# Layer 0's attention with VectorE in the program's order, adaLN's loads a slot ahead, and the query rotation cut in three slots

## The chip, the cores and the metric

The kernel runs on one core of one Trainium2 chip. The metric is the device time of one execution in microseconds; smaller is better. A core has five instruction streams that matter here: TensorE (PE, with its weight loads shown apart as PEld), VectorE (DVE), ScalarE (ACT), GpSimd (POOL) and SyncE (SP), which issues nearly all of the DMAs.

## The reference

Two layers of a diffusion transformer over 1024 latent tokens and 256 context tokens of width 1024. Each layer modulates its input with an adaLN vector, mixes tokens, gates, projects, and adds the residual under a layer norm. Layer 0 is multi-head latent attention with 16 heads, layer 1 differential attention. Cut to what this change touches:

```python
shift, scale, gate = adaln(c, ada_w[i], ada_b[i])          # silu(c) @ w + b, also for c_ctx
h = x * (1.0 + scale[:, None, :]) + shift[:, None, :]
# layer 0
q_lat, kv_lat, k_pe, gate = jnp.split(t @ w_in, splits, axis=-1)
q = (rms_norm(q_lat, g_qa) @ w_qb).reshape(bsz, n, 16, 64 + 32)
kv = (rms_norm(kv_lat, g_kva) @ w_kvb).reshape(bsz, n, 16, 64 + 64)
q_pe = apply_rope(q_pe, cos, sin); k_pe = apply_rope(k_pe, cos, sin)   # latent tokens only
o = softmax(q k^T * 96**-0.5) v          # latent queries see 1280 keys, context queries the 256 context keys
x = layer_norm(4**0.25 * x + gate * ((o * silu(gate)) @ out_w), ln_g, ln_b)
```

The adaLN products of layer 1 (2 x 1024 by 1024 x 3072) depend on nothing but the conditioning vectors, so they can be computed at any time before layer 1 needs them.

## The kernel before

The program is written in Python and its instructions are put in order by a planner, which has a cost model, gives earlier instructions the higher priority and lets an engine take a later instruction that is ready when an earlier one isn't. Inside `tc.manual_schedule(engines=...)` the engines named keep the program's order instead; all others are still planned. Before the change, the attention of layer 0 names TensorE alone (`MAN = 'P'`, L36).

Precision is kept by splitting: each operand is a high part and a low part, and a product is three matmuls (`mm3`, L185). `split16` (L180) makes the parts: ScalarE writes the high one, then VectorE the low one from the same source and the high one.

**Ahead of the attention.** The latents are projected (up to about 165 us), then the gates of layer 0 are computed in 40 tiles (`gate_tile`, L284), with a side generator beside them, `beside_gates` (L475): it splits the up-projection weights (`up_weights`, L346, with the key rotation and the column norms `col_norms`, L380, which bound the scores), and then computes four chunks of adaLN (`ada_dve`, L431). From 250 to 282 us the values are made (`prod_v0`, L537), and head 0's keys, queries and first row maxima.

**adaLN on VectorE** (`ada_dve`). A chunk is 512 columns of one layer's weight. For each of eight row blocks SP loads 128 x 512 weights into an `adw` buffer (256 KB, L437), and VectorE adds the block, times a column of the conditioning, into one or two accumulators (L441 for the first block, L443 for the others). Each block is one slot of the generator (`yield`). Then two more slots: TensorE sums an accumulator over the partitions (L450 or L462) and VectorE adds the bias (L452 or L463). The attention's generator `ada` has four chunks of layer 1: two with two accumulators (latent and context) and two with one.

**The attention** (L779 to L797). A head has three blocks of queries: `b` = 0 and 1 with 512 latent queries each, and `b` = 2 with the 256 context queries. A unit (`units0`, L709) is one block of queries against two tiles of 128 keys: five units for each latent block, one for the context block. A unit takes six score matmuls into a pair of PSUM banks (L723 to L725), on ScalarE an exponential and a copy to f16 (L667, L668), on GpSimd the low part by a subtraction (L669, both inputs in SBUF), and two units later (`LAG = 2`) twice twelve value matmuls (L735 to L738), in two parts (`retire(0)`, `retire(1)`). After the last unit of a block `fin` divides by the sum on VectorE (L746, L747).

The softmax needs the row maximum of each query beforehand, in the query operand itself: `max0` (L636) computes it in six slots for a latent block. Four slots each multiply 128 queries by 1024 keys (L647) and reduce them on VectorE (L649, 128 x 1024). The fifth does the context keys (L653, L654) and joins the maxima (`ng`, L655). The sixth turns them into rows by a matmul (L658), and VectorE writes them into the query operand (L659, `qH` for a latent block, `qcH` for the context block). A context block has two slots.

Keys and queries of the next head come from `prod_k` (L588) and `prod_q` (L605). Every second head projects keys and plain queries for two heads; every fourth head (while heads 3, 7 and 11 run) projects the rotated part of the queries for four heads, runs `rope` (L250: a shuffle, two products, a sum on VectorE, each 128 x 1024) and splits it. Copies by SP then place the rows of one head (L599, L600, L631, L632).

`run_step` (L690) weaves all this. For each unit it issues the scores, then the first half of the unit's list of side slots, the first twelve value matmuls, the second half of the list, and the other twelve. The list is made from `sides` in order, each generator with its number of slots per unit. One run is block 0 of a head (five units), a second run blocks 1 and 2 (six units). The scores, maxima and projections all take their PSUM from one tag of three pairs, `pair()` (L91), in turn, so a matmul can wait for the reduce or the exponential that read the same pair last. The last head has two runs of its own, with the loads of the output weight beside them (`load_outw`, L756, VectorE's part in L761).

After the attention come the output projection of layer 0, layer 1's attention and its output, up to 1941 us; the change doesn't touch them.

Of the kernel before, what the change touches and what calls it, by code (L numbers as in the profile page):

```python
# [9 lines left out]
F32 = mybir.dt.float32  # L10
F32R = mybir.dt.float32r
# [6 lines left out]
P = 128  # L18
# [16 lines left out]
WAT = ((1, 4, 8, 12, 15), (24, 28, 33, 38, 42))  # L35
MAN = 'P'  # L36
MAN1 = 'P'
HP = 0
# [15 lines left out]
def hybrid_kernel(  # L54
# [194 lines left out]

    def rope(ps, n, cos, sin, sw, r):  # L250
        dve.stream_shuffle(sw[:, :n], ps, SWAP16)
        dve.tensor_tensor(r[:, :n], ps, cos, op=ALU.mult)
        dve.tensor_tensor(sw[:, :n], sw[:, :n], sin, op=ALU.mult)
        dve.tensor_tensor(r[:, :n], r[:, :n], sw[:, :n], op=ALU.add)
        return r[:, :n]

# [89 lines left out]
    def up_weights(pa):  # L346
# [15 lines left out]
        for c0, n in CHUNKS:  # L362
            c = slice(c0, c0 + n)
            kt = pa.tile([ROPE, 512], F32, tag="kt", name=nm("kt"))
            sp.dma_start(kt[:, :n], kp_d[:, c])
            if c0 < SEQ:
                tabs = []
                for j in range(2):
                    tb = pa.tile([ROPE, 512], F32, tag=f"ktab{j}", name=nm("ktab"))
                    sp.dma_start(tb, cs0[j, :ROPE, c])  # L370
                    tabs.append(tb)
                rope(kt, n, tabs[0], tabs[1], rot(pa, [ROPE, 512], F32, "rsw"), kr[:, c])
            else:
                dve.tensor_copy(kr[:, c], kt[:, :n])
            yield
# [4 lines left out]
        def col_norms(dst, parts, n):  # L380
            wsq = pa.tile([P, 2, 512], F32R, tag="wsq", name=nm("wsq"))
            for c0 in range(0, n, 512):
                for j, f in enumerate(parts):
                    f(wsq[:, j, :], slice(c0, c0 + 512))
                yield
                bk = bank("c")
                for j, f in enumerate(parts):
                    pe.matmul(bk, onr, wsq[:, j, :], start=j == 0, stop=j == len(parts) - 1)
# [16 lines left out]
        for i, n in ((0, KVL), (1, KVL), (2, 4 * QL)):  # L405
# [25 lines left out]
    def ada_dve(tile_, bk_, chunks):  # L431

        for layer, pc in chunks:
            acc = [tile_(f"acc{s}") for s in range(1 if layer and pc > 3 else 2)]
            for k in range(KT):
                w = tile_("adw")
                sp.dma_start(w, ada_w[layer, k * P:(k + 1) * P, pc * 512:(pc + 1) * 512])  # L437
                for s, a_ in enumerate(acc):
                    ck = sc[:, 2 * k + s:2 * k + s + 1]
                    if k == 0:  # L440
                        dve.tensor_scalar_mul(a_, w, ck)  # L441
                    else:
                        dve.scalar_tensor_tensor(a_, w, ck, a_, op0=ALU.mult, op1=ALU.add)  # L443
                yield
# [37 lines left out]
    with spool("p0g") as pg:  # L482
# [14 lines left out]
        for _ in side:  # L497
# [107 lines left out]
    def prod_q(h, b):  # L605
# [3 lines left out]
        if h % 4 == 0 and b != 1:  # L609
# [169 lines left out]
    for h in range(H0):  # L779
        last = h == H0 - 1  # L780
        even, quad = (h + 1) % 2 == 0, (h + 1) % 4 == 0
        if last:
# [4 lines left out]
            run_step(units0(h, 0) + units0(h, 2), [(max0(h, 2), (1, 0, 1)), (max0(h, 1), (0, 1, 1, 1, 2, 1)),  # L787
                                                   (load_outw(oH, oL, lambda: w0("ows")), (1, 2, 2, 2, 1))])
            run_step(units0(h, 1), [])
# [599 lines left out]
```

## Time and profile before

| What | Value |
|---|---|
| median of 3 runs | 1940.24 us (1938.42 to 1947.27) |
| the profiled execution's own time | 1943.4 us |
| its span, first to last instruction | 1941.5 us |
| mean granted TensorE clock | 0.966 |
| TensorE busy in layer 0's attention, 350 to 385 us | 33.90 of 35 us |
| VectorE busy there | 21.73 of 35 us |
| GpSimd busy there | 26.92 of 35 us |

The page of the profile gives busy time by engine, then the span in 40 slices, then the costliest groups of instructions. A row in order of time reads: start, duration, engine, line of the kernel, operation, output <- inputs, shapes, and in brackets the idle time of the engine just before it with what ended it. "x2" at the end of a row says that two instructions are merged in it. A row of the table by windows has, after the window and its length, the busy time of TensorE, its weight loads, VectorE, ScalarE and GpSimd, each with its count of instructions, then the granted clock (1.00 is full speed), the DMA share and GB/s. A row of a group ends with its busy time, the mean of one in ns, and the idle time before them.

### The profile page before, as it was taken

What the parts mean: (1) busy time and instruction counts of PE and PEld (TensorE: products, weight loads), DVE (VectorE), ACT (ScalarE), POOL (GpSimd) and SP (SyncE); (2) the same over time, 40 slices, a digit from 0 to 9 for tenths busy, and PEclk for the clock granted to TensorE, in tenths of its full rate; (3) what the DMA queues carried; (4) which work ended last, traced back from release to release, by engine and by line L of the source; (5) the groups of instructions that cost most, each with busy time, mean ns of one, the idle gap of its engine ahead of it and who ended that gap; (6) DMA issues with size and microseconds to landing.
All of it is one profiled execution on the core that took longest, in us unless ns stands there. A gap on an engine that the chain in (4) does not pass through costs nothing. (4 is left out here: it accounts for less than half of the span.)

```text
span 1941.5 us, 36839 instructions
## 1 busy us (share of the span) xinstructions
PE 1748.3 (90%) x14460; PEld 1348.4 (69%) x14460; DVE 1294.9 (67%) x2211; ACT 1037.9 (53%) x2100; POOL 904.3 (47%) x755
## 2 busy tenths in 40 slices
PE   8889979989899899788889998999999999995997
PEld 2889945656556565566668787878787878783666
DVE  1535577585665758436643868696868787868775
ACT  2532157767677688711114565656666666665331
POOL 2442036757667676756563425242424242416222
PEclk9999989999999999989989999999999999997999
DMA  7345531121211213143233212111111121205331
GB/s 248 106 115 155 170 91 43 41 81 24 75 42 40 62 37 107 34 181 126 93 109 91 62 39 56 47 48 49 51 50 50 44 56 34 58 18 194 105 111 61
DMA packets 116365, 155.40 MB, mean 80 GB/s; under 512 B 14448, under 2 KB 85712, under 8 KB 116192
## 3 DMA queue, kind: packets, MB, share of 16 engines
q1 hardware_dynamic: 110432, 147.80, 25.1%
q10 hardware_dynamic: 5760, 5.25, 0.8%
q8 instruction: 114, 1.87, 0.4%
q14 instruction: 59, 0.48, 0.1%
HBM read 99.18 MB, written 27.08 MB: 65 GB/s over the span
## 5 line engine op out<-in xcount | busy, mean ns | idle before, releaser
L669 POOL TENSOR_TENSOR pl<-p,ph 128x1024 f16<-128x1024 f32 (+1 forms) x176 | 367.6, 2094 | 171.5 <-ACT ph L668 160.0
L1110 ACT ACTIVATE p<-ps_b,mx 128x512 f32<-128x512 f32 (+1 forms) x384 | 232.8, 626 | 46.1 <-DVE mx L1107 45.6
L667 ACT ACTIVATE p<-ps_a,esc 128x1024 f32<-128x1024 f32 (+1 forms) x176 | 189.1, 1074 | 119.9 <-PE ps_a L725 113.1
L649 DVE TENSOR_REDUCE mx<-ps_a 128x1 f32<-128x1024 f32 x128 | 155.1, 1220 | 102.2 <-PE ps_a L647 102.2
L183 DVE SCALAR_TENSOR_TENSOR pl<-ps_b,lcf,ph 128x512 f16<-128x512 f32 (+1 forms) x192 | 123.4, 657 | 110.7 <-ACT ph L182 109.3
L668 ACT CAST ph<-p 128x1024 f16<-128x1024 f32 (+1 forms) x176 | 177.1, 1006 | 5.5
L1104 DVE TENSOR_REDUCE mx<-ps_b 128x1 f32<-128x512 f32 x256 | 165.9, 677 | 0.3 <-PE ps_b L1088 0.2
L186 PE MATMUL ps_b<-h1H,wH 128*128 128x512 f32 (+1 forms) x384 | 150.0, 391 | 17.8 <-ACT p L1110 16.1
L738 PE MATMUL ps_d<-Vh,pl 128*128 128x65 f16 x1344 | 150.8, 195 | 7.4 <-POOL pl L669 6.1
L186 PE MATMUL ps_b<-wH,h1H 128*128 128x256 f32 x512 | 156.2, 305 | 0.0
L735 PE MATMUL ps_d<-Vh,ph 128*128 128x65 f16 x1344 | 154.2, 196 | 0.0
L737 PE MATMUL ps_d<-Vl,ph 128*128 128x64 f16 x1344 | 152.7, 193 | 0.0
L187 PE MATMUL ps_b<-wL,h1H 128*128 128x256 f32 x512 | 146.5, 286 | 0.0
L188 PE MATMUL ps_b<-wH,h1L 128*128 128x256 f32 x512 | 146.4, 286 | 0.0
L182 ACT ACTIVATE ph<-ps_b,lcf 128x512 f16<-128x512 f32 (+1 forms) x192 | 120.5, 640 | 41.3 <-PE ps_b L1123 41.3
L188 PE MATMUL ps_b<-h1H,wL 128*128 128x512 f32 (+1 forms) x384 | 139.1, 362 | 3.4 <-POOL wL L178 3.4
L178 POOL TENSOR_TENSOR wL<-ws,wH 128x512 fp32r<-128x512 f32 x64 | 91.3, 1428 | 106.5 <-PE ps_b L187 59.0
L735 PEld LDWEIGHTS <-ph 128*128 128x128 f16 x1344 | 124.6, 98 | 22.6 <-issue 5.6
L187 PE MATMUL ps_b<-h1L,wH 128*128 128x512 f32 (+1 forms) x384 | 138.5, 361 | 0.0
L737 PEld LDWEIGHTS <-ph 128*128 128x128 f16 x1344 | 125.2, 99 | 16.0 <-issue 0.3
L723 PE MATMUL ps_a<-qH,KH 100*128 100x512 f16 x320 | 123.0, 384 | 13.4 <-DVE qH L659 7.6
L1087 PE MATMUL ps_b<-KS,QS 128*128 128x512 f16 (+1 forms) x384 | 128.9, 353 | 3.6 <-ACT p L1110 2.5
(344 smaller groups left out, 5424.1 us busy)
## 6 DMA issues: line engine op xcount, KB each, us to landing
adw<-in_ada_w SPq DMA_DIRECT2D x64, 256.0 KB
ws<-in_dw SPq DMA_DIRECT2D x64, 256.0 KB
g<-sg_d SPq DMA_DIRECT2D x18, 512.0 KB
adaw<-in_ada_w SPq DMA_DIRECT2D x16, 512.0 KB
sg_d<-gg ACTq DMA_DIRECT2D x40, 128.0 KB
o<-o_d SPq DMA_DIRECT2D x10, 512.0 KB
o_d<-op SPq DMA_DIRECT2D x7, 640.0 KB
xt<-in_xT SPq DMA_DIRECT2D x16, 256.0 KB
```

Of the source, the lines that this page charges most:

```text
L186: pe.matmul(ps, aH, bH, start=start, stop=False, skip_group_check=skip)
L187: pe.matmul(ps, aH, bL, start=False, stop=False, skip_group_check=skip)
L188: pe.matmul(ps, aL, bH, start=False, stop=stop, skip_group_check=skip)
L649: dve.tensor_reduce(mx[:, t, 0:1], ps, axis=AX.X, op=ALU.max)
L667: act.activation(p32[:, :n], st, AF.Exp, scale=esc0)
L668: act.copy(ph[:, :n], p32[:, :n])
L669: pool.tensor_tensor(pl[:, :n], p32[:, :n], ph[:, :n], op=ALU.subtract)
L735: pe.matmul(pv[:, t, :], ph[:, ts], Vh[:, k, h, :], start=(k == kcs[0] and t == 0), stop=False, skip_group_check=True)
L737: pe.matmul(pv[:, t, :V0], ph[:, ts], Vl[:, k, h, :], start=False, stop=False, skip_group_check=True)
L738: pe.matmul(pv[:, t, :], pl[:, ts], Vh[:, k, h, :], start=False, stop=(k == NT - 1), skip_group_check=True)
L1104: dve.tensor_reduce(mx[:, 2 + 2 * m + i:3 + 2 * m + i], b, axis=AX.X, op=ALU.max, negate=True)
L1110: act.activation(p[m][:, c0:c0 + n], b, AF.Exp, bias=nb, scale=sc1, accum_out=sm[:, 2 + 3 * m + i:3 + 3 * m + i])
```

## The change

- `MAN0 = 'PD'`: in the two runs of heads 0 to 14 VectorE too keeps the program's order. The last head's runs, and everything outside the runs, keep `MAN`.
- `ada_dve` loads one block ahead: a first slot only loads, and each later slot issues the load of the next block before it computes on its own. `adw` has three buffers instead of two in the attention.
- In both runs `ada` moves from the first to the last place of `sides`. In the third unit of the first run and the third and fifth of the second, its slot so comes after the maxima, and the first half of the list holds a maximum slot more.
- `rope` becomes a generator with two slots: shuffle and first product, then second product and sum. With the split behind them the rotated queries take three slots; the units of heads 3, 7 and 11 get (2, 2, 2, 1, 1) slots of `kq` instead of (2, 2, 2, 0, 0), so that plain queries are projected in the fourth unit and copied in the fifth (before: both in the third).
- In `up_weights`, `col_norms` takes single tiles of 512 columns in two buffers instead of one tile of two; the table buffers of the key rotation grow from 512 to 640 columns, and the low half of the rotated keys is staged in one of them.

```diff
+MAN0 = 'PD'
...
     def rope(ps, n, cos, sin, sw, r):
+
         dve.stream_shuffle(sw[:, :n], ps, SWAP16)
         dve.tensor_tensor(r[:, :n], ps, cos, op=ALU.mult)
+        yield
         dve.tensor_tensor(sw[:, :n], sw[:, :n], sin, op=ALU.mult)
         dve.tensor_tensor(r[:, :n], r[:, :n], sw[:, :n], op=ALU.add)
-        return r[:, :n]
+        yield
...
-                    tb = pa.tile([ROPE, 512], F32, tag=f"ktab{j}", name=nm("ktab"))
+                    tb = pa.tile([ROPE, 640], F32, tag=f"ktab{j}", name=nm("ktab"))[:, :512]
...
-            wsq = pa.tile([P, 2, 512], F32R, tag="wsq", name=nm("wsq"))
             for c0 in range(0, n, 512):
-                for j, f in enumerate(parts):
-                    f(wsq[:, j, :], slice(c0, c0 + 512))
+                wsq = [pa.tile([P, 512], F32R, tag="wsq", bufs=2, name=nm("wsq")) for _ in parts]
+                for w_, f in zip(wsq, parts):
+                    f(w_, slice(c0, c0 + 512))
...
-        kl_ = pa.tile([P, 2, 512], F32R, tag="wsq", name=nm("wsq")).rearrange(
-            "p a b -> p (a b)").bitcast(F16)[:ROPE, :NTOK]
+        kl_ = pa.tile([ROPE, 640], F32, tag="ktab1", name=nm("ktab")).bitcast(F16)
...
-        for layer, pc in chunks:
+        def load(i):
+            layer, pc = chunks[i // KT]
+            k = i % KT
+            w = tile_("adw")
+            sp.dma_start(w, ada_w[layer, k * P:(k + 1) * P, pc * 512:(pc + 1) * 512])
+            return w
+
+        ahead = [load(0)]
+        yield
+        for i, (layer, pc) in enumerate(chunks):
             acc = [tile_(f"acc{s}") for s in range(1 if layer and pc > 3 else 2)]
             for k in range(KT):
-                w = tile_("adw")
-                sp.dma_start(w, ada_w[layer, k * P:(k + 1) * P, pc * 512:(pc + 1) * 512])
+                if i * KT + k + 1 < len(chunks) * KT:
+                    ahead.append(load(i * KT + k + 1))
+                w = ahead.pop(0)
...
-            "ows": ([P, D], F32, 2), "adw": ([P, 512], F32, 2), "acc0": ([P, 512], F32, 1),
+            "ows": ([P, D], F32, 2), "adw": ([P, 512], F32, 3), "acc0": ([P, 512], F32, 1),
...
-                src = rope(src, pn, cosA, sinA, w0("rsw"), w0("rr"))
+                rr = w0("rr")
+                yield from rope(src, pn, cosA, sinA, w0("rsw"), rr)
+                src = rr
...
-    def run_step(units, sides):
-
-        with tc.manual_schedule(engines={ENG[c] for c in MAN}):
+    def run_step(units, sides, man_=MAN0):
+
+        with tc.manual_schedule(engines={ENG[c] for c in man_}):
...
             kq = chain(prod_k(h + 1), prod_q(h + 1, 0))
-            run_step(units0(h, 0), [(ada, (0, 0, 1)), (max0(h, 1), (1, 1, 2, 1, 1)), (max0(h, 2), (0, 1, 0, 1)),
-                                    (kq, (2, 2, 1 + quad, 0, 0) if even else (2,))])
+            run_step(units0(h, 0), [(max0(h, 1), (1, 1, 2, 1, 1)), (max0(h, 2), (0, 1, 0, 1)),
+                                    (kq, ((2, 2, 2, 1, 1) if quad else (2, 2, 1)) if even else (2,)),
+                                    (ada, (0, 0, 1))])
             qs = chain(prod_q(h + 1, 1), prod_q(h + 1, 2))
-            run_step(units0(h, 1) + units0(h, 2), [(ada, (0, 0, 1, 0, 1)), (max0(h + 1, 0), (1, 1, 1, 2, 1)),
-                                                   (qs, (1, 1 + quad, 0, 1) if even else (2,))])
+            run_step(units0(h, 1) + units0(h, 2), [(max0(h + 1, 0), (1, 1, 1, 2, 1)),
+                                                   (qs, (1, 1 + quad, 0, 1) if even else (2,)),
+                                                   (ada, (0, 0, 1, 0, 1))])
```

The last head's two calls pass `MAN`.

More of the change, by code (lines that the diff above doesn't have):

```diff
@@ L368, in up_weights @@
                 for j in range(2):
-                    tb = pa.tile([ROPE, 512], F32, tag=f"ktab{j}", name=nm("ktab"))
+                    tb = pa.tile([ROPE, 640], F32, tag=f"ktab{j}", name=nm("ktab"))[:, :512]
                     sp.dma_start(tb, cs0[j, :ROPE, c])
                     tabs.append(tb)
-                rope(kt, n, tabs[0], tabs[1], rot(pa, [ROPE, 512], F32, "rsw"), kr[:, c])
+                for _ in rope(kt, n, tabs[0], tabs[1], rot(pa, [ROPE, 512], F32, "rsw"), kr[:, c]):
+                    pass
             else:
@@ L380, in col_norms @@
         def col_norms(dst, parts, n):
-            wsq = pa.tile([P, 2, 512], F32R, tag="wsq", name=nm("wsq"))
             for c0 in range(0, n, 512):
-                for j, f in enumerate(parts):
-                    f(wsq[:, j, :], slice(c0, c0 + 512))
+                wsq = [pa.tile([P, 512], F32R, tag="wsq", bufs=2, name=nm("wsq")) for _ in parts]
+                for w_, f in zip(wsq, parts):
+                    f(w_, slice(c0, c0 + 512))
                 yield
                 bk = bank("c")
-                for j, f in enumerate(parts):
-                    pe.matmul(bk, onr, wsq[:, j, :], start=j == 0, stop=j == len(parts) - 1)
+                for j, w_ in enumerate(wsq):
+                    pe.matmul(bk, onr, w_, start=j == 0, stop=j == len(parts) - 1)
                 dve.tensor_reduce(vm[:, 6:7], bk, axis=AX.X, op=ALU.max)
@@ L787, in hybrid_kernel @@
             run_step(units0(h, 0) + units0(h, 2), [(max0(h, 2), (1, 0, 1)), (max0(h, 1), (0, 1, 1, 1, 2, 1)),
[L788 to L789 removed]
+                                                   (load_outw(oH, oL, lambda: w0("ows")), (1, 2, 2, 2, 1))], MAN)
+            run_step(units0(h, 1), [], MAN)
         else:
             kq = chain(prod_k(h + 1), prod_q(h + 1, 0))
[L792 to L793 removed]
+            run_step(units0(h, 0), [(max0(h, 1), (1, 1, 2, 1, 1)), (max0(h, 2), (0, 1, 0, 1)),
+                                    (kq, ((2, 2, 2, 1, 1) if quad else (2, 2, 1)) if even else (2,)),
+                                    (ada, (0, 0, 1))])
             qs = chain(prod_q(h + 1, 1), prod_q(h + 1, 2))
[L795 to L796 removed]
+            run_step(units0(h, 1) + units0(h, 2), [(max0(h + 1, 0), (1, 1, 1, 2, 1)),
+                                                   (qs, (1, 1 + quad, 0, 1) if even else (2,)),
+                                                   (ada, (0, 0, 1, 0, 1))])
     flush()
```

## The prediction

> **What bounds the kernel now.** I read the page first, then the table of busy time by windows, then the order of time on TensorE and VectorE in layer 0's attention.
>
> ```profile
> PE 1748.3 (90%) x14460; PEld 1348.4 (69%) x14460; DVE 1294.9 (67%) x2211; ACT 1037.9 (53%) x2100; POOL 904.3 (47%) x755
> 250.00:282.00 32.00, 23.76 (x97) 16.64 (x97) 24.83 (x26) 18.75 (x20) 12.62 (x7) 0.89 0.34 99
> 350.00:385.00 35.00, 33.90 (x406) 21.87 (x404) 21.73 (x31) 28.49 (x28) 26.92 (x15) 1.00 0.17 45
> 404.00:408.00 4.00, 3.82 (x26) 2.03 (x26) 3.25 (x4) 1.51 (x2) 1.33 (x1) 0.60 0.31 94
> ```
>
> TensorE is the bound (90% of the span). The change reaches the gates' stage (up to 250 us), its end (250 to 282) and the attention (282 to about 815). In a good stretch of the attention TensorE is busy 33.9 of 35 us at full clock; at the stage's start it has 23.8 of 32 at clock 0.89. In order of time, the long waits of TensorE there name VectorE:
>
> ```profile
> 277.79 0.60 PE L653 MATMUL ps_a<-KH,qH 96*128 96x256 f16 x4 [2.02 <-DVE mx L649]
> 280.84 0.27 PE L658 MATMUL ps_a<-idr,ng 128*4 128x128 f32 x1 [2.46 <-DVE ng L655]
> 404.18 0.38 PE L723 MATMUL ps_a<-qH,KH 100*128 100x512 f16 x1 [2.85 <-DVE qH L659]
> ```
>
> What VectorE did in front of them is adaLN, in bursts. A first chunk has run by 307, then comes nothing of it for 88 us, then the next chunk:
>
> ```profile
> 303.86 3.28 DVE L443 SCALAR_TENSOR_TENSOR acc<-adw,sc,acc 128x512 f32<-128x512 f32 x2
> 395.27 0.87 DVE L441 TENSOR_SCALAR acc<-adw,sc 128x512 f32<-128x512 f32 x2
> L443 DVE SCALAR_TENSOR_TENSOR acc<-adw,sc,acc x98: 714/747/2675, 168.3 to 644.7; 128x512 f32<-128x512 f32 x98
> L443 DVE SCALAR_TENSOR_TENSOR acc<-adw,sc,acc 128x512 f32<-128x512 f32 x39 | 46.1, 1197 | 7.3 <-DMA adw<-in_ada_w 7.1
> ```
>
> So the planner fills every idle moment of VectorE with steps that the program meant for later heads, and row maxima wait behind them. A head's pace shows in the times at which its query rows get their maxima (L659: qcH is once a head, qH twice):
>
> ```profile
> 281.48 0.74 DVE L659 SCALAR_TENSOR_TENSOR qH<-ps_a,sh,selt 4x512 f16<-4x512 f32 x1
> 331.67 0.47 DVE L659 SCALAR_TENSOR_TENSOR qcH<-ps_a,sh,selt 2x256 f16<-2x256 f32 x1
> 360.23 0.48 DVE L659 SCALAR_TENSOR_TENSOR qcH<-ps_a,sh,selt 2x256 f16<-2x256 f32 x1
> 399.54 0.48 DVE L659 SCALAR_TENSOR_TENSOR qcH<-ps_a,sh,selt 2x256 f16<-2x256 f32 x1
> 436.58 0.48 DVE L659 SCALAR_TENSOR_TENSOR qcH<-ps_a,sh,selt 2x256 f16<-2x256 f32 x1
> 469.15 0.48 DVE L659 SCALAR_TENSOR_TENSOR qcH<-ps_a,sh,selt 2x256 f16<-2x256 f32 x1
> 497.67 0.48 DVE L659 SCALAR_TENSOR_TENSOR qcH<-ps_a,sh,selt 2x256 f16<-2x256 f32 x1
> 545.14 0.48 DVE L659 SCALAR_TENSOR_TENSOR qcH<-ps_a,sh,selt 2x256 f16<-2x256 f32 x1
> 560.84 0.74 DVE L659 SCALAR_TENSOR_TENSOR qH<-ps_a,sh,selt 4x512 f16<-4x512 f32 x1 [0.41 <-PE ps_a L658]
> 607.03 0.47 DVE L659 SCALAR_TENSOR_TENSOR qcH<-ps_a,sh,selt 2x256 f16<-2x256 f32 x1
> 637.91 0.47 DVE L659 SCALAR_TENSOR_TENSOR qcH<-ps_a,sh,selt 2x256 f16<-2x256 f32 x1
> 676.63 0.48 DVE L659 SCALAR_TENSOR_TENSOR qcH<-ps_a,sh,selt 2x256 f16<-2x256 f32 x1
> 705.90 0.48 DVE L659 SCALAR_TENSOR_TENSOR qcH<-ps_a,sh,selt 2x256 f16<-2x256 f32 x1
> 739.26 0.48 DVE L659 SCALAR_TENSOR_TENSOR qcH<-ps_a,sh,selt 2x256 f16<-2x256 f32 x1
> 771.05 0.48 DVE L659 SCALAR_TENSOR_TENSOR qcH<-ps_a,sh,selt 2x256 f16<-2x256 f32 x1
> ```
>
> The qcH rows are heads 1 to 14, a few left out. An even head takes 28.5 us undisturbed (469.15 to 497.67, 331.67 to 360.23), an odd one 32.6 (436.58 to 469.15), the one after a rotation 29.3 (676.63 to 705.90), and one that makes rotated queries without a burst 38.7 (637.91 to 676.63).
>
> **What goes: the bursts.** Against those paces: the stretch 281.48 to 331.67 is 50.2 us, the same kind of stretch without adaLN (560.84 to 607.03) 46.2: 4.0. Head 4 (399.54 to 436.58) has 37.0 for 29.3: 7.7. Head 7 (497.67 to 545.14) has 47.5 for 38.7: 8.8, part of it a slow clock. Head 10 (607.03 to 637.91) has 30.9 for 28.5: 2.4. Ahead of 282 the two waits of 2.02 and 2.46 stand directly behind adaLN; in program order none of it can come before head 0, so 4.0 of these 4.5 go. Sum 26.9, between 22.9 (without the stage's start) and 27.4. Head 14 (739.26 to 771.05) has 31.8 for 28.5, filled with the last head's weight splits (L761); these stay with the planner, but it may no longer slip them between VectorE's fixed instructions. Between 0 and 3.3, I take 1.5. **Gain 28.4 us.**
>
> **What comes: the same steps, spread.** adaLN's 41 slots now lie three to a head, in heads 0 to 13: (a) third unit of the first run, (b) third and (c) fifth unit of the second. Sixteen slots compute on two accumulators, sixteen on one, the rest are loads, matmuls or empty. In order, each stands between two row maxima. What it costs there, from head 2, which has no adaLN now, and from one adaLN step that met GpSimd:
>
> ```profile
> 508.34 2.67 DVE L443 SCALAR_TENSOR_TENSOR acc<-adw,sc,acc 128x512 f32<-128x512 f32 x1
> 508.34 2.12 POOL L669 TENSOR_TENSOR pl<-p,ph 128x1024 f16<-128x1024 f32 x1 [0.32 <-ACT ph L668]
> 356.07 2.35 DVE L649 TENSOR_REDUCE mx<-ps_a 128x1 f32<-128x1024 f32 x2 [0.50 <-PE ps_a L647]
> 358.02 2.13 POOL L669 TENSOR_TENSOR pl<-p,ph 128x1024 f16<-128x1024 f32 x1 [0.59 <-ACT ph L668]
> 358.97 1.23 DVE L654 TENSOR_REDUCE mx<-ps_a 128x4 f32<-128x1024 f32 x1 [0.54 <-PE ps_a L653]
> 361.04 0.24 PE L658 MATMUL ps_a<-idr,ng 128*4 128x128 f32 x1
> 361.46 0.20 PE L738 MATMUL ps_d<-Vh,pl 128*128 128x65 f16 x1
> L655 DVE TENSOR_REDUCE ng<-mx 128x4 fp32r<-128x8 f32 x31 | 5.0, 160 | 0.9
> 657.11 1.23 DVE L649 TENSOR_REDUCE mx<-ps_a 128x1 f32<-128x1024 f32 x1 [3.05 <-PE ps_a L647]
> ```
>
> A step of 0.75 us (median above) took 2.67, because GpSimd's subtraction started with it: it ended 0.55 after GpSimd did (510.46). Now place (a). The two maxima of the unit end at 358.42; GpSimd runs from 358.02 to 360.15. The step behind the maxima would end at 360.70, with two accumulators at 361.45. The maximum that stands at 358.97 starts then and, with 0.16 us for the joined maximum (L655), lets TensorE have L658 at 362.1 or 362.85 instead of 361.04: 1.0 or 1.8 us. That is for an even head; an odd one has its maximum later, behind a query projection, and I take half. By the slots' count (a) has five double steps (heads 1, 2, 4, 5, 6) and three single ones outside the rotating heads (8, 9, 12): 0.9+1.8+1.8+0.9+1.8+1.0+0.5+1.0 = 9.7. In (b) only one maximum is ahead, the step meets the end of GpSimd's work; I take 0.5 for each of five double steps, 2.5. In (c) VectorE has nothing urgent behind it: before the next head's first maximum it is idle for 3.05 us (row 657.11), which hides even a double step; nothing, and a full step if that idle time were gone. Moving adaLN last also moves the joined maximum's matmul in the second run ahead of twelve value matmuls, 0.42 us by the rows 361.04 and 361.46, fifteen times: between 0 and 6, mostly lent, as TensorE would do the twelve anyway; I take 1. **Cost 13 us**, from 0 (all of it in idle time) to 46.1 (the group row's whole busy time).
>
> The loads a slot ahead come at least two units before use, some 5 us (11 units in 28.5 us). Today's waits for them are 7.3 us of VectorE's idle time in the bursts (the L443 group), counted there already. On SP's queue a load is still one issue per step, now earlier by a slot; with three buffers the one it overwrites was read two slots before, so SP does not stand and the copies of queries and keys behind it (L631, L599) go on time: nothing, and at most those same waits if a load came late. The splits of keys and plain queries wait for ScalarE in order too, and the maxima, `fin` and their buffers queue behind them; in the undisturbed odd head of 32.6 us these stand in the same order, so I take 0. In the gates' stage the planner still orders VectorE, and the split `wsq`, the larger `ktab` and adaLN's extra first slot lie beside the gates' matmuls: nothing, and one step of 0.75 us if these were gone.
>
> **The rotation in three slots** (heads 3, 7, 11). Now in head 11:
>
> ```profile
> 668.83 1.23 DVE L254 TENSOR_TENSOR rr<-rr,rsw 128x1024 f32<-128x1024 f32 x1
> 669.15 2.92 POOL L669 TENSOR_TENSOR pl<-p,ph 128x1024 f16<-128x1024 f32 x1 [3.64 <-ACT ph L668]
> L183 DVE SCALAR_TENSOR_TENSOR stpL<-rr,qsc,stpH 128x1024 f16<-128x1024 f32 x3 | 5.4, 1809 | 0.0
> 670.09 1.15 ACT L182 ACTIVATE stpH<-rr,qsc 128x1024 f16<-128x1024 f32 x1 [1.08 <-DVE rr L254]
> 675.57 0.38 PE L723 MATMUL ps_a<-qH,KH 100*128 100x512 f16 x1
> ```
>
> Today the four rotation steps run in a row, L254 ends at 670.06. In order, two maxima (2.35) come between its halves; the second half then starts at 670.0, meets GpSimd's 2.1 us from 669.15 and so ends near 673.4 (671.3 and two steps of a little over 1 us behind it). Then the in-order queue waits for ScalarE's 1.15 (stpH), to 674.6, splits (1.8 by the group's mean, most of it GpSimd's lock; I take 1.7), to 676.3, takes a single adaLN step in heads 7 and 11, to 677.0, and only then the maximum (1.23) whose buffer the scores of the fifth unit need: 678.3 for 675.57 today, 2.8 later; 2.1 in head 3. In all **7.7 us**. The other way, if the maxima ahead of the rotation free TensorE sooner, it is 0; the other end adds a clock fall: after the 2.85 us wait at 404.18 the clock is 0.60 over 4 us, 1.6 us lost, three times, 12.5. I take 7.7, the rows' own sum.
>
> [...]
>
> **Sum:** -28.4 + 13.2 + 7.7 = -7.5 us. The profiled execution is 1943.4 (span 1941.5 and 1.9 around it), so 1935.9; it lies 3.2 above the median of 1940.24, and for the median I say **1933**.
>
> **Rivals.** *The spread is free:* the steps and the rotation fall into VectorE's idle time, as places (c) do. For it: VectorE is busy 21.7 of 35 us in the good window; against it: place (a)'s rows. Costs 0: 1940.2-28.4 = **1912**. *In single file it is slower:* at (a) and (b) each step's whole time lands on the maximum behind it, GpSimd's subtraction and VectorE's step excluding each other in every unit. Ten double and nine single steps there at 1.2 us an accumulator are 35 us, with the rotation's upper end 47.5, less 28.4: +19, **1959**. It decides once the costs pass 28.4. For it: GpSimd is busy 26.9 of 35 us; against it: today's bursts cost 26.9 us for 46.1 us of steps. [...] *The order hardly changes:* the planner already had nearly this order and the bursts' time is the rotation's: **1940**. Against it: 88 us without a step.
>
> **Chances.** Forecast 0.45 (1924 to 1942), free 0.27, single file 0.20, no change 0.08. A measurement of this kernel tells about 0.5% from no change, 9.7 us: 1930.5 to 1949.9. Of the forecast 0.20 lies below that, 0.25 inside. Faster 0.20+0.27 = 0.47; same 0.25+0.08+0.02 = 0.35; slower 0.18. The range reaches from 1910, just under the free case, to 1955, which leaves out the upper part of single file.
>
> **What would show it.** Right: L443 of the attention spread over heads 0 to 13, no two steps of different slots adjacent; L441 after 282; head 4 near 29 to 31 us; clock near 1.0 where it is 0.60 now; L658 waits of 1 to 2 us in heads 1 to 6; in the rotating heads one wait of 2 to 4 us of L723 for L654. Wrong: heads 2 and 6 still at 28.5 (free), or all heads from 1 to 12 two us longer (single file), or rotating heads above 42.

## The result and the profile after

The change makes the kernel slower: 1957.14 us (median of 5, 1951.97 to 1960.06) against 1941.18 for the kernel before beside it, a ratio of 1.0070 (95% interval 1.0043 to 1.0097). The forecast was 1933, range 1910 to 1955. The profiled execution took 1952.52 us (span 1950.4), near the low end of the five; its mean clock is 0.964, and that of the three executions above 1957 is 0.960 to 0.962.

On the page TensorE's busy time is what it was, within 2.4 us; the span is 8.9 longer.

```profile
PE 1750.7 (90%) x14460; PEld 1345.5 (69%) x14460; DVE 1302.0 (67%) x2211; ACT 1038.6 (53%) x2100; POOL 904.8 (46%) x755
```

The pace by heads, in order of time on VectorE. L659 is now L674 (the lines behind the new ones shift: L443 is L456, L658 is L673, L723 is L738, L761 is L776). As in the prediction, "head n" is the stretch that ends in its qcH row; the rows are those of heads 1 to 8 and 11 to 14, behind the first qH:

```profile
274.77 0.74 DVE L674 SCALAR_TENSOR_TENSOR qH<-ps_a,sh,selt 4x512 f16<-4x512 f32 x1 [0.45 <-PE ps_a L673]
...
323.19 0.48 DVE L674 SCALAR_TENSOR_TENSOR qcH<-ps_a,sh,selt 2x256 f16<-2x256 f32 x1
353.93 0.48 DVE L674 SCALAR_TENSOR_TENSOR qcH<-ps_a,sh,selt 2x256 f16<-2x256 f32 x1
396.03 0.48 DVE L674 SCALAR_TENSOR_TENSOR qcH<-ps_a,sh,selt 2x256 f16<-2x256 f32 x1
431.25 0.48 DVE L674 SCALAR_TENSOR_TENSOR qcH<-ps_a,sh,selt 2x256 f16<-2x256 f32 x1
469.05 0.48 DVE L674 SCALAR_TENSOR_TENSOR qcH<-ps_a,sh,selt 2x256 f16<-2x256 f32 x1
500.06 0.48 DVE L674 SCALAR_TENSOR_TENSOR qcH<-ps_a,sh,selt 2x256 f16<-2x256 f32 x1
542.12 0.48 DVE L674 SCALAR_TENSOR_TENSOR qcH<-ps_a,sh,selt 2x256 f16<-2x256 f32 x1
574.92 0.48 DVE L674 SCALAR_TENSOR_TENSOR qcH<-ps_a,sh,selt 2x256 f16<-2x256 f32 x1
...
676.98 0.48 DVE L674 SCALAR_TENSOR_TENSOR qcH<-ps_a,sh,selt 2x256 f16<-2x256 f32 x1
711.20 0.48 DVE L674 SCALAR_TENSOR_TENSOR qcH<-ps_a,sh,selt 2x256 f16<-2x256 f32 x1
743.67 0.48 DVE L674 SCALAR_TENSOR_TENSOR qcH<-ps_a,sh,selt 2x256 f16<-2x256 f32 x1
781.80 0.47 DVE L674 SCALAR_TENSOR_TENSOR qcH<-ps_a,sh,selt 2x256 f16<-2x256 f32 x1
```

Two cuts, at the first qH and at the qcH of head 13, divide a span in three:

| Kernel | until the first qH | heads 0 to 13 | from there to the end | span |
|---|---|---|---|---|
| before | 281.48 | 457.78 | 1202.2 | 1941.5 |
| the change | 274.77 | 468.90 | 1206.7 | 1950.4 |
| difference | -6.7 | +11.1 | +4.5 | +8.9 |
| forecast | -4.0 | -2.0 | -1.5 | -7.5 |

The bursts did go (heads 4 and 7: 35.2 and 42.1 us for 37.0 and 47.5), but heads 2, 3, 5, 6, 8, 12 and 14 became longer, head 5 by 5.2 us, head 12 by 5.0 and head 14 by 6.3 (1, 9 and 11 by less than 1). By the prediction's own signs: heads 3 and 7 take 42.1 us, just above its line of 42 for the heads that make rotated queries, and head 4 takes 35.2 where 29 to 31 would have been right; but by no means all heads from 1 to 12 are two us longer.

Two kinds of wait are new. TensorE's rows: L673 waits for the joined maximum (0.86 to 1.79 us seven times between 323 and 712, of which two rows stand here, and twice 2.4), and in each rotating head (3, 7 and 11) the scores wait for L669.

```profile
354.04 0.22 PE L673 MATMUL ps_a<-idr,ng 128*4 128x128 f32 x1 [1.62 <-DVE ng L670]
370.93 0.22 PE L673 MATMUL ps_a<-idr,ng 128*4 128x128 f32 x1 [2.43 <-DVE ng L670]
395.85 0.38 PE L738 MATMUL ps_a<-qH,KH 100*128 100x512 f16 x1 [2.84 <-DVE mx L669]
446.61 0.22 PE L673 MATMUL ps_a<-idr,ng 128*4 128x128 f32 x1 [2.45 <-DVE ng L670]
500.17 0.22 PE L673 MATMUL ps_a<-idr,ng 128*4 128x128 f32 x1 [1.79 <-DVE ng L670]
541.95 0.38 PE L738 MATMUL ps_a<-qH,KH 100*128 100x512 f16 x1 [3.24 <-DVE mx L669]
676.80 0.59 PE L738 MATMUL ps_a<-qH,KH 100*128 100x512 f16 x1 [3.52 <-DVE mx L669]
```

And the clock. The table by windows, with the granted clock in the third number from the end, shows from head 1 on five short falls and one long, all but one (516 to 520) at the end of such a wait or right behind it (another fall is under way when head 0 starts, at clock 0.50 until 280.42 us, as it is before, until 288.71):

```profile
355.00:359.00 4.00, 3.88 (x26) 1.94 (x25) 0.69 (x2) 1.39 (x2) 1.96 (x1) 0.57 0.14 37
396.00:400.00 4.00, 4.00 (x34) 2.27 (x33) 2.51 (x3) 1.87 (x2) 0.00 (x0) 0.57 0.18 46
447.00:452.00 5.00, 5.00 (x58) 3.43 (x54) 2.88 (x3) 1.35 (x3) 2.85 (x2) 0.66 0.17 32
516.00:520.00 4.00, 4.00 (x36) 2.72 (x35) 2.15 (x7) 1.30 (x2) 2.67 (x2) 0.58 0.02 4
543.00:548.00 5.00, 5.00 (x55) 3.09 (x54) 2.06 (x3) 2.93 (x3) 2.13 (x1) 0.66 0.36 100
676.00:684.00 8.00, 7.20 (x50) 3.60 (x50) 3.52 (x6) 2.64 (x3) 2.06 (x1) 0.57 0.32 80
```

A window's length times one less its clock is what it lost: 4 x 0.43 = 1.7 us for a short fall, 8 x 0.43 = 3.4 for the long one, 11.9 in all. Before, heads 1 to 13 lost 6.8 in three falls (391 to 395, 404 to 409, 517 to 525).

### The profile page after: what moved, and what is told of

It is laid out like the page before. It is cut to its first block, busy times and chain, and to the rows that moved or that the text cites. A ratio compares the mean times of both kernels' runs of the same rounds, so it can differ in the third digit from the quotient of the medians.

```text
span 1950.4 us, 36828 instructions
## 1 busy us (share of the span) xinstructions
PE 1750.7 (90%) x14460; PEld 1345.5 (69%) x14460; DVE 1302.0 (67%) x2211; ACT 1038.6 (53%) x2100; POOL 904.8 (46%) x755
## 5 line engine op out<-in xcount | busy, mean ns | idle before, releaser
L738 PE MATMUL ps_a<-qH,KH 100*128 100x512 f16 x320 | 125.7, 393 | 15.2 <-DVE mx L669 9.6
```

## The experiments

Each ratio is to the kernel before, timed on the same chip; times of different groups are compared through these ratios.

**Which part of the change is it?** First the theory that the fixed order makes the loss, from both sides.

`order alone`: the kernel before with VectorE in order in heads 0 to 14.

```diff
-    def run_step(units, sides):
+    def run_step(units, sides, man_='PD'):
-        with tc.manual_schedule(engines={ENG[c] for c in MAN}):
+        with tc.manual_schedule(engines={ENG[c] for c in man_}):
```

> The kernel before with the fixed order alone: VectorE in the program's order in heads 0 to 14, adaLN first in a unit with its load in its own slot, the rotation in one slot. Theory: adaLN's steps stand ahead of the maxima, wait for their own load too, and the rotation's four steps stand in a row, so it is as slow as the change or slower, 1957 to 1985 us. Rival (the order is harmless, the other parts cost): 1935 to 1945.

1948.44 us, ratio 1.0000 (0.9984 to 1.0016). `planned`: all of the change but the order (`MAN0 = 'P'`).

> The changed kernel with one letter taken back: VectorE is planned again in the runs of heads 0 to 14, all else of the change stays. Theory (the fixed order costs: adaLN's steps meet GpSimd's subtraction between two row maxima, the rotation's chain holds up the maximum behind it): adaLN runs in bursts again and the time goes back to 1930 to 1945 us. Rival (the load ahead, the third buffer, the lists of side slots or the rotation's slots cost it, the order does not): it stays at 1950 to 1960.

1956.97 us, 1.0050 (1.0029 to 1.0071). So the order by itself is neutral as a whole, and the rest of the change is slow without it: my first theory fell. In the planned run the bursts are back, up to six steps in a row, and the second run of units of each rotating head starts 2.9 us late, as the scores wait for the query rows. A burst on VectorE, then TensorE in head 7:

```profile
423.27 5.94 DVE L456 SCALAR_TENSOR_TENSOR acc<-adw,sc,acc 128x512 f32<-128x512 f32 x6
```

```profile
549.43 0.39 PE L738 MATMUL ps_a<-qH,KH 100*128 100x512 f16 x1 [2.93 <-DVE qH L674]
```

`rotation alone`: the kernel before with the rotation in three slots and nothing else.

```diff
         dve.tensor_tensor(r[:, :n], ps, cos, op=ALU.mult)
+        yield
         dve.tensor_tensor(sw[:, :n], sw[:, :n], sin, op=ALU.mult)
...
-                                    (kq, (2, 2, 1 + quad, 0, 0) if even else (2,))])
+                                    (kq, ((2, 2, 2, 1, 1) if quad else (2, 2, 1)) if even else (2,))])
```

> The kernel before with the rotation of queries in three slots and the new numbers of slots, and nothing else of the change; VectorE stays planned. Theory R (the rotation's slots are what makes the planned version slow): the plain queries are projected one unit later in heads 3, 7 and 11, so the second run of heads 3, 7 and 11 begins with a wait of about 2.9 us on each of three rows, as the run with the planned order showed, plus a clock fall of 1.7 after each: 3 x (2.9 + 1.7) = 14 us slower, ratio 1.006 to 1.008. Rival L (adaLN's place in the list and its loads ahead make it slow): ratio 0.999 to 1.002, the three waits under 1 us.

1956.94 us, 1.0052 (1.0032 to 1.0071), as much as the whole planned run. Heads 4, 8 and 12 take 43.1, 34.9 and 33.5 us for 37.0, 29.3 and 29.3 before. Two of the three waits are there at the size expected, the first is 1.65. VectorE in head 11 shows why: the planner puts a maximum between the two steps of the rotation's second half, both meet GpSimd (2.24 and 2.60 us for steps of 1.2), and the plain queries, now projected a unit later, are split behind them.

```profile
683.69 2.24 DVE L254 TENSOR_TENSOR rsw<-rsw,sinA 128x1024 f32<-128x1024 f32 x1
685.85 1.21 DVE L658 TENSOR_REDUCE mx<-ps_a 128x4 f32<-128x1024 f32 x1
686.99 2.60 DVE L255 TENSOR_TENSOR rr<-rr,rsw 128x1024 f32<-128x1024 f32 x1
...
692.00 1.28 DVE L183 SCALAR_TENSOR_TENSOR stqL<-ps_a,qsc,stqH 128x1024 f16<-128x1024 f32 x1
693.31 0.74 DVE L663 SCALAR_TENSOR_TENSOR qH<-ps_a,sh,selt 4x512 f16<-4x512 f32 x1
```

`adaLN last alone`: the kernel before with `ada` last in both lists.

> The kernel before with adaLN last in the lists of the units in place of first, and nothing else of the change; VectorE stays planned. Theory L: the bursts of L443 move behind maxima and meet a unit's start, waits of about 3 us as at 279 and 295 us in the run with the planned order, ratio 1.004 to 1.008. Theory R: with VectorE planned the place in the list is only a priority, ratio 0.998 to 1.002.

1945.58 us, 1.0004 (0.9987 to 1.0021): with VectorE planned, the place in the list changes nothing that these runs can tell.

**In the fixed order, which part?** `rotation undone`: the change with `rope` in one slot and (2, 2, 1 + quad, 0, 0). `adaLN first`: the change with `ada` first in both lists again.

> The change with the rotation of queries in one slot again and the old numbers of slots; the order, adaLN's last place and the loads ahead stay. Theory P (in the fixed order adaLN's place alone costs): 1.006 to 1.008, as the change. Theory R (the rotation's slots alone cost): 0.999 to 1.001, as the run with the order alone. Both parts: 1.002 to 1.005, with heads 4, 8 and 12 some 2 us each below the change's 35.2, 32.8 and 34.2, and the waits of L673 of 1.6 and 2.4 us in heads 2, 4 and 6 kept.

> The change with adaLN first in the units' lists again, all else kept. Theory P: 0.999 to 1.001, waits of 0.9 to 1.3 us of L668 in heads 1 to 6 in place of L673's 0.9 to 2.4. Theory R: 1.006 to 1.008. Both parts: 1.002 to 1.005.

Rotation undone: 1951.06 us, 1.0023 (1.0005 to 1.0041). adaLN first: 1949.28 us, 1.0008 (0.9995 to 1.0022). Each alone brings back most of the 0.7%, so neither theory of one cause holds. The two parts cost more together (0.0070) than the sum of what each costs alone in this order (0.0023 and 0.0008); the excess of 0.4% is hardly larger than what the three intervals leave open (0.35%). One place where they meet is the last step of this chain, the change's head 11 on VectorE: behind the split stands an adaLN step, and only then the maximum for which the scores wait.

```profile
668.50 2.10 DVE L256 TENSOR_TENSOR rsw<-rsw,sinA 128x1024 f32<-128x1024 f32 x1
...
673.09 1.86 DVE L184 SCALAR_TENSOR_TENSOR stpL<-rr,qsc,stpH 128x1024 f16<-128x1024 f32 x1 [1.22 <-ACT stpH L183]
674.88 0.74 DVE L456 SCALAR_TENSOR_TENSOR acc<-adw,sc,acc 128x512 f32<-128x512 f32 x1
675.54 1.21 DVE L669 TENSOR_REDUCE mx<-ps_a 128x4 f32<-128x1024 f32 x1
```

That wait is 3.52 us in the change and 2.83 with adaLN first, where the step is not in the chain:

```profile
672.58 0.58 PE L738 MATMUL ps_a<-qH,KH 100*128 100x512 f16 x1 [2.83 <-DVE mx L669]
```

**What does the place of adaLN's steps cost?** `idle places`: the change with the steps in the fifth unit of the first run and the fifth and sixth of the second. `first run idle` and `second run idle` take one line of it each.

```diff
-                                    (ada, (0, 0, 1))])
+                                    (ada, (0, 0, 0, 0, 1))])
...
-                                                   (ada, (0, 0, 1, 0, 1))])
+                                                   (ada, (0, 0, 0, 0, 1, 1))])
```

> The change with adaLN's three slots of a head moved to where VectorE idles: the fifth unit of the first run, the fifth and sixth of the second, each behind the last slot of the maxima. Theory (the waits of 1 to 2.4 us of L673 and the clock falls behind them come from the places between maxima): 10 to 16 us less than the change, 1941 to 1947. Rival (the rotating heads and head 14 alone make the loss): 1952 to 1957.

> The change with adaLN's slot of the first run moved from the third to the fifth unit; the second run's two slots stay. Both moved gave 0.9926 where the change has 1.0070: 1.44% or 28 us to share. By the prediction's sizes (9.7 us for the first run's slot, 2.5 for the second run's) four fifths of it go here: 0.995 to 0.997, and the waits of 2.4 us of L673 in heads 2 and 4 stay. Rival, that the second run's double steps, each met by two of GpSimd's operations, cost more than the first run's: 1.000 to 1.004.

> The change with adaLN's slots of the second run moved from the third and fifth to the fifth and sixth unit; the first run's slot stays. By the prediction's sizes: 1.003 to 1.005, with waits of 0.9 to 1.8 us of L673 in heads 1 to 12 kept and the two of 2.4 us gone. Rival: 0.995 to 0.999.

Idle places: 1934.40 us, 0.9926 (0.9908 to 0.9944), faster than the kernel before. First run's slot moved alone: 1936.80, 0.9963 (0.9949 to 0.9976). Second run's alone: 1949.10, 1.0016 (1.0003 to 1.0030). Of the change's 1.0070 the first takes 1.07% or 21 us, the second 0.54% or 10, both together 1.44% or 28, where 10 to 16 had been expected; the change's own interval, 5 us either way, goes into each of these. The place of these steps is the largest single cost. In the idle places, four steps run one after the other where VectorE would stand, and the even head behind takes 29.07 us:

```profile
440.97 5.68 DVE L456 SCALAR_TENSOR_TENSOR acc<-adw,sc,acc 128x512 f32<-128x512 f32 x4
...
460.67 0.48 DVE L674 SCALAR_TENSOR_TENSOR qcH<-ps_a,sh,selt 2x256 f16<-2x256 f32 x1
489.74 0.48 DVE L674 SCALAR_TENSOR_TENSOR qcH<-ps_a,sh,selt 2x256 f16<-2x256 f32 x1
```

**The rotation's slots in the fixed order.** `rotation later` is the change with (2, 2, 1, 2, 1) in place of (2, 2, 2, 1, 1); the other two have the idle places as well, one with the rotation undone, one with the rotation later.

> The change with the split of the rotated queries moved from the third to the fourth unit of heads 3, 7 and 11, behind that unit's maximum. Theory (the scores of the fifth unit wait 2.8 to 3.5 us for the maximum behind that split, and the clock falls after it): these three waits shrink to about 1 us and 6 to 12 us go, 1945 to 1951. Rival (VectorE is simply full there, so the wait moves to the query rows): 1954 to 1959.

> The change with adaLN's steps in the fifth units (0.9926) and the rotation in one slot. If the rotation's slots cost half a per cent in the fixed order too: 0.987 to 0.990. If they cost only with VectorE planned: 0.992 to 0.994, the rotating heads with waits of 3.5 us of the scores for the row maxima as in the run with the order alone.

> The change with adaLN's steps in the fifth units and the rotation's fourth unit given the second slot; the last head as in the change. In the run with these two and the last head in order, the attention's last head began 12.7 us earlier than with the places alone, 6 us of it by head 14, and the last head and what follows took 11.7 us more: without the ordered last head 6 to 7 us of it stay: ratio 0.988 to 0.991, some 1925 where the kernel before has 1944. If the two don't add, 0.9926 stays.

Rotation later: 1953.64, 1.0023 (1.0002 to 1.0044), 9 us less than the change by the ratios and so within the first theory's 6 to 12, though the two intervals leave some 6 us either way. Idle places with the rotation undone: 1930.90, 0.9915 (0.9890 to 0.9940), not to be told from 0.9926. Idle places with the rotation later: 1927.25, 0.9905 (0.9888 to 0.9922), the lowest ratio, called the best version from here on, although its interval overlaps those of 0.9915 and 0.9926. The scores of the rotating heads no longer wait for a maximum but for the query rows, and only 1.64 to 1.66 us, as here in head 7.

```profile
528.20 0.38 PE L738 MATMUL ps_a<-qH,KH 100*128 100x512 f16 x1 [1.64 <-DVE qH L674]
```

**The last heads.** Head 14's 6.3 us stand behind the output weight's splits, which the planner slips between VectorE's fixed instructions. VectorE and TensorE in the change:

```profile
760.04 2.96 DVE L776 SCALAR_TENSOR_TENSOR oL<-ows,usc,oH 128x1024 fp32r<-128x1024 f32 x1
```

```profile
763.22 0.27 PE L673 MATMUL ps_a<-idr,ng 128*4 128x128 f32 x1 [3.78 <-DVE ng L670]
```

`last ordered` is the change with the last head's two calls without `MAN`; `all three` has the idle places, the rotation later and this; `splits last` has them too, with the splits' slots in the last run.

```diff
-                                                   (load_outw(oH, oL, lambda: w0("ows")), (1, 2, 2, 2, 1))], MAN)
-            run_step(units0(h, 1), [], MAN)
+                                                   ])
+            run_step(units0(h, 1), [(load_outw(oH, oL, lambda: w0("ows")), (2, 2, 2, 1, 1))])
```

> The change, with the last head's two runs in the program's order on VectorE as well. If the six us that head 14 lost (38.13 against 31.79) come from the last head's splits, which the planner slips between head 14's fixed instructions, they go: 1957 less 4 to 8, a ratio to the kernel before of 1.002 to 1.005, and head 14 at 32 us. If head 14 is slow by its own order, the time stays at 1.007.

> The change with adaLN's steps in the fifth units (the run of that name was 0.9926), the rotation's fourth unit given the second slot (0.995 against the change), and the last head in order. If the three add: the first gave 0.9926, the second takes some 5 us, the third 4 to 8: 1918 to 1926 where the kernel before has 1941, ratio 0.988 to 0.992. If they lie beside one another, 0.9926 stays.

> The change with adaLN's steps in the fifth units, the rotation's second slot in the fourth unit (0.9905 together), and the last head in the program's order on VectorE with the splits of the output weight moved into its last run, behind all row maxima. If head 14's lost time is these splits standing between maxima, it goes and does not come back in the last head as with the last head in order alone: 6 to 10 us less than 0.9905, so 0.985 to 0.988, head 14 near 29.5 us and no wait of L673 over 2 us in the last head. If the splits then hold up the projection behind the attention by their 13 to 20 us: 0.993 to 0.998.

Last ordered: 1962.01, 1.0076 (1.0058 to 1.0094). All three: 1935.63, 0.9942 (0.9922 to 0.9961). Splits last: 1927.35, 0.9910 (0.9892 to 0.9928). None of the three brought the time that it was to bring. In the first, head 14 takes 29.6 us for 38.1, so the splits were what held it up, and the last head loses as much: its own maxima now wait behind the splits, TensorE 6.41 us in one place:

```profile
817.00 0.27 PE L673 MATMUL ps_a<-idr,ng 128*4 128x128 f32 x1 [6.41 <-DVE ng L670]
```

With the splits behind all maxima head 14 takes 31.7, and in the last run value matmuls wait 2.13 us for GpSimd. GpSimd itself had waited for ScalarE's copy, and ScalarE had stood 1.80 us for a load of the output weight, ahead of its own part of the splits:

```profile
793.26 1.15 ACT L775 ACTIVATE oH<-ows,usc 128x1024 fp32r<-128x1024 f32 x1 [1.80 <-DMA ows<-in_out_w]
797.76 0.24 PE L753 MATMUL ps_d<-Vh,pl 128*128 128x65 f16 x1 [2.13 <-POOL pl L684]
```

From the end of head 13 to the end of the span it is 1203.2 us there and 1202.7 without it (idle places with the rotation later), so nothing is won: in each of the places tried, something waits for the splits or their loads.

## Why the prediction was wrong

It went wrong in both large terms. If the best version (span 1922.0, all of the change but two sets of slots) is taken for the change without its costs, the profiled executions split the result: the change wins 19.5 us (1941.5 - 1922.0) and loses 28.4 (1950.4 - 1922.0), +8.9; the forecast had 28.4 won and 20.9 lost, -7.5.

Where the time of heads 0 to 13 goes can be added up. The waits are the sum of the brackets of TensorE's rows, the clock loss is length times one less the granted clock, here with the fall at the start of head 0. In all seventeen traces what is then left is 413.8 to 417.1 us, so these two make the differences:

| Kernel | heads 0 to 13 | TensorE's waits | clock lost |
|---|---|---|---|
| before | 457.8 | 30.7 | 10.4 |
| order alone | 463.9 | 36.1 | 12.0 |
| the change | 468.9 | 38.8 | 14.8 |
| idle places | 450.6 | 29.0 | 7.6 |
| the best version | 444.8 | 24.8 | 6.2 |

- **What goes: the bursts (28.4 us), the step that failed first.** They went, as the heads show, and heads 0 to 13 should have become 22.9 us shorter without the new costs. The best version's are 12.9 shorter (444.84 us), and those of the order alone, where the bursts are gone too, 6.1 longer (463.90). The step took the paces of the planner's undisturbed heads (28.5, 29.3, 32.6) for what every head would have. In the fixed order they are not all reached even with adaLN in idle places: heads 5, 8 and 12 take 34.4, 31.6 and 31.7 us (9 takes 33.0). Of the 41.1 us of waits and lost clock before, the best version keeps 31.0; the forecast needed some 18. The order alone has 48.1. In it the waits for joined maxima behind the bursts (L658, 9.0 us) are gone, but the product with the context keys (L653) and the scores (L723) wait 18.6 us for row maxima, 7.7 before, and a projection waits 4.0 us at 394.83 for adaLN's bias step (L452), which stands behind the rotation's split. So the fixed order, with adaLN's steps in it, has a price about as large as the bursts', which agrees with 1.0000 for the order alone. The prediction's "so I take 0" for the splits that wait in order was too low as well, by little: TensorE's waits for tiles of the splits and the rotation (`stkL`, `stqL`, `rr`) sum to 6.7 us in the change and 4.1 before. In the idle places 1.2 to 1.3 us of wait for a row maximum is left in each of heads 3 and 5 (behind the four steps shown above in head 5), and the rotating heads' waits.
- **The start.** Forecast -4.0, measured -6.7 in this pair of executions. The matmul that waits 3.4 us for the split of head 0's keys starts at 245.60 instead of 250.59, so 5.0 of the 6.7 arose ahead of 250, in the gates' stage, which I had taken at nothing. But single executions scatter here: the first qH comes between 278.4 and 285.4 us in the four traces whose program ahead of the attention is the old one (before, the order, adaLN last and the rotation alone), and between 273.5 and 279.7 in the thirteen with the new one. The means are 281.7 and 276.0, 5.7 apart; which edit makes that was not tested.
- **The steps spread, place (a), 9.7 us.** As waits right: rows of 0.86, 1.62, 1.63, 0.86, 1.79, 0.96 and 0.97 us, 8.7 in all; steps on two accumulators cost 1.6 to 1.8 in even heads and 0.86 in odd ones, steps on one 1.0. As time it is short by half: 21 us by the experiment, which also takes the step out of the rotating heads. In its profiled execution heads 0 to 13 are 17.6 us shorter than the change's, 9.4 of it waits and 7.0 clock.
- **Place (b), 2.5 us, the term mis-sized most.** I had one maximum ahead and none behind. Two maxima stand behind it, and a double step met two of GpSimd's operations: the first step (1.04 us) lasts until 0.55 us after GpSimd's operation has ended at 440.91; GpSimd's next one starts at 441.23, just before the second step does, and this step (2.62 us) lasts until 0.55 us after that one's end too. TensorE waits 2.45 us at 446.61, and 2.43 at 370.93. By the experiment the place is worth 10 us; in its profiled execution heads 0 to 13 are 5.3 us shorter, 0.6 of it waits (others came for the two that went) and 5.0 clock. The rows of VectorE and of GpSimd in the change:

```profile
440.42 3.58 DVE L456 SCALAR_TENSOR_TENSOR acc<-adw,sc,acc 128x512 f32<-128x512 f32 x2
443.92 1.21 DVE L664 TENSOR_REDUCE mx<-ps_a 128x1 f32<-128x1024 f32 x1
445.06 1.21 DVE L669 TENSOR_REDUCE mx<-ps_a 128x4 f32<-128x1024 f32 x1
```

```profile
438.78 2.13 POOL L684 TENSOR_TENSOR pl<-p,ph 128x1024 f16<-128x1024 f32 x1 [0.32 <-ACT ph L683]
441.23 2.22 POOL L684 TENSOR_TENSOR pl<-p,ph 128x1024 f16<-128x1024 f32 x1 [0.32 <-ACT ph L683]
```

- **The clock, left out.** The waits of (a) and (b) sum to 13.6 us against a forecast of 13.2 with the matmul moved ahead, yet moving the steps away saved 28. In the two profiled executions (spans 1950.4 and 1931.8) heads 0 to 13 differ by 18.3 us: 9.8 of waits (the 13.6 are gone, smaller ones such as the 1.2 to 1.3 in heads 3 and 5 have come), and 7.2 of clock lost. The prediction had the price of a fall (1.6) only as an upper end for the rotation. The medians differ by more than the profiled pair, and the change's longer executions have the lower clock; that the rest of the 28 is clock too is not shown.
- **The rotation, 7.7 us.** The size was right in the change: undoing it brings 1.0070 to 1.0023, 9 us. The working was not: undone, the scores wait 2.90 to 2.92 us for the same maximum, against 2.84, 3.24 and 3.52, and beside the idle places nothing measurable is left of it (0.9915 and 0.9926). No run shows that most of the split's 1.8 us is GpSimd's, as the working had it: in the change's head 11 it takes 1.86 us (673.09 above), of which 1.08 lie behind the end of GpSimd's subtraction (671.04 to 673.87). So that 9 us is near 7.7 is luck. A price of the rotation shows only together with adaLN's steps in their places behind the maxima, or with a planned VectorE (1.0052); the waits of these three rows grew by 0.9 us in all, and what makes the rest of the 9 us was not taken apart.
- **Place (c), loads ahead, zero each.** Not contradicted: with the loads ahead, the order and the three slots, but adaLN first, it is 1.0008. The loads alone were not run.
- **Head 14, 1.5 us won.** It lost 6.3 us, and the whole stretch from the end of head 13 on lost 4.5. The prediction said that the planner may no longer slip the splits between VectorE's fixed instructions. It still does: the one at 760.04 shown above stands between the unit's last maximum (758.91) and the joined maximum (762.92). Moving the splits wins nothing.

Of the rivals, *the order hardly changes* has the time of the order alone by another road: the order changes much, and its parts cancel. *Single file* names the right mechanism for the cost, the steps' time landing on the maxima behind them, though not in every unit: of the change's 42 steps of L456 in heads 0 to 13, 24 start while GpSimd subtracts and end 0.55 us behind it (0.89 to 2.65 us each), and 18 take 0.74. That its 1959 us lies near the measured time is luck: it set a cost of 47.5 against a gain of 28.4, and by the split above they are 28.4 and 19.5.

## What to carry to other kernels

The fastest stretch that a planner reached by itself is no floor that a fixed order will reach everywhere; price the order alone, as a run of its own, before crediting it with what the disturbed stretches lose. In a fixed order, filler work goes where the next instruction of its engine waits for nothing urgent: here two numbers in a list were worth 1.4%, more than the whole change. Price a wait on TensorE as the wait and the chance of a clock fall behind it (1.7 us here).

## What the runs showed that was not expected

The change's clock falls from head 1 on lost portions of 1.7 us (3.41 us at clock 0.50), and a wait's length alone does not tell whether one follows. With the first run's steps in idle places, the same wait of 2.85 us occurs at 531.74 with no fall and at 663.09 with one. TensorE's rows, then stretches of 3.41 us around them (the first number behind the length is TensorE's busy time):

```profile
531.74 0.38 PE L738 MATMUL ps_a<-qH,KH 100*128 100x512 f16 x1 [2.85 <-DVE mx L669]
663.09 0.38 PE L738 MATMUL ps_a<-qH,KH 100*128 100x512 f16 x1 [2.85 <-DVE mx L669]
```

```profile
527.22:530.63 3.41, 1.67 (x18) 1.20 (x17) 2.19 (x3) 2.15 (x2) 2.25 (x1) 1.00 0.04 10
530.63:534.04 3.41, 2.27 (x31) 1.39 (x31) 3.28 (x5) 0.74 (x1) 0.00 (x0) 1.00 0.11 29
660.34:663.75 3.41, 0.66 (x4) 0.30 (x4) 3.33 (x4) 0.67 (x1) 0.48 (x1) 1.00 0.07 19
663.75:667.16 3.41, 3.41 (x31) 2.03 (x30) 2.78 (x3) 1.83 (x2) 0.00 (x0) 0.50 0.19 48
```

The two differ in where the wait lies. In the change the falls start at 355.5, 396.5, 447.7, 515.9, 543.2 and 676.4 us, which is 12, 15, 20, 8 and 39 times 3.41 us apart, and each lasts 3.41 us or twice that, at clock 0.50 (the first from 355.51 to 358.93). Cut into stretches of that length from the start of its fall (663.75), the trace with the two equal waits has the one at 663.09 fill most of one stretch, in which TensorE is busy 0.66 us, and half clock follows; the wait at 531.74 is shared by two stretches with 1.67 and 2.27 us busy, and none follows. Of the change's stretches in heads 1 to 13, cut from 355.51 in the same way, six have TensorE busy for less than half, and behind five of them the clock falls; the closest are 1.68 us busy (352.10 to 355.51, with a fall) and 1.64 (369.16 to 372.57, without). Of all others at full clock one is followed by a fall: the stretch before 515.9, busy 3.14 us, in which most is adaLN's one-column matmuls (L463); why it falls there was not tested.

The shortest wait with a fall right behind it was 1.62 us (354.04 in the change, window 355 to 359); in the stretch that holds it, 352.10 to 355.51, TensorE was busy 1.68 us.

A pair of adaLN's steps met two of GpSimd's subtractions: the second subtraction started just before the second step did (441.23 above), and the pair took 3.58 us, where two steps of 0.74 would take 1.5.
